# Spreading the norm's factor of each token over the partitions: by a store to DRAM and a repeating load, in the place of products of ones with diagonals

## The chip, the cores and the metric

The kernel runs on one core of one Trainium2 chip. The metric is the device time of one execution in microseconds (us); the kernel before takes 1041.21 us, the median of three runs (1041.09 to 1044.4).

## What is computed

One step of a hybrid decoder layer. A prompt of 2048 tokens and 8 single decode tokens, each of width 1024, go through one mixer that has two groups of heads on the same normalised input. What matters here is the first line of it: the norm, and the projections behind it.

```python
def rmsnorm(x, g):
    xf = x.astype(jnp.float32)
    y = xf * lax.rsqrt(jnp.mean(xf * xf, axis=-1, keepdims=True) + NORM_EPS)
    return (y * g.astype(jnp.float32)).astype(x.dtype)
...
def mixer_layer(x, pos, s_ret, s_hg, norm_g, w_in, ret_g, hg_g, lb, w_out):
    B, L, _ = x.shape
    h = rmsnorm(x, norm_g)
    p = (h @ w_in).astype(jnp.float32)
    rq, rk, rv, rg, hq, hf, hi, hgate = jnp.split(p, 8, axis=-1)
    ...
    y = x + o_cat @ w_out
```

Each token has one factor, 1/sqrt(mean(x*x) + eps). The activations lie transposed on the chip, with the width on the 128 partitions and the tokens along a row. A factor that belongs to a token is therefore the same on all partitions and changes along the row, while the sums of squares come out with one token on each partition. Bringing the factors from one layout into the other is what the change is about.

## The kernel before

**Pairs and steps.** The first 570 us project the 2048 tokens with three sets of weights. The tokens are cut into eight blocks of 256 (two chunks of 128). `TOK` lists 24 turns, eight for each set of weights; the program calls turn i "pair i", since it makes two chunks. Pairs 0 and 1 are plain products. From pair 2 on, `v_pair` (L393) makes a 2x2 block product out of seven smaller ones, in seven steps numbered 0 to 6 (`CHAIN`, L364). A step is 12 matmuls of 128x512: each float is split into a high and a low part (`hi_lo`, L114: ScalarE writes `ab_h`, VectorE writes `ab_l`), and high*high, high*low and low*high are added up. Of the names, `pv4a`, `pv4b`, `pv4c` are the PSUM banks of pair 4.

**What a pair needs.** `tok_load` (L235) brings the raw activations `xr` of a block, two halves of 512 KB. `tok_ops` (L306) multiplies them in place by the norm's gain and the spread factor `rb` (L313, eight instructions of 128x256), splits them into `ab_h` and `ab_l`, and makes four sums S1 to S4 (L328 to L331), which `s_split` (L338) splits into `s..h` and `s..l`. Scaled activations and sums are stored for the later sets (`a_dram` L321, `s_dram` L334). All this is done for pair i+1 while pair i is multiplied. What a pair makes leaves as `vo` (`emit`, L402): `vo440` after step 1 of pair 4, `vo451` after step 4 (a copy by ScalarE, L412, and an addition by VectorE, L413), `vo441` after step 5, `vo450` after step 6. Each goes out by a store to `v_dram` (L354).

**The factor before.** `stats_load` and `stats_sum` load the tokens once more, untransposed (`xn`), and square and sum them on ScalarE (L267). GpSimd adds the halves and takes the power -0.5 (L277, L111, L112); the result is a column of `rs_all` with one token on each partition. `spread_dg` (L284) makes two diagonal matrices `dg` of it on VectorE. `spread` (L290) multiplies ones by them on TensorE (L293, `prs`), so that every partition gets the row of factors, and VectorE copies the row out of PSUM to `rb` (L295). That is done for eight blocks: for pairs 2 to 7, each during the pair before it, and for pairs 10 and 11, which are the first to meet the blocks of the plain pairs. The eight decode tokens have their own small copy of the scheme (`decode_dg` L620, `decode_spread` L623).

**The gate.** In pairs 2 to 5 and 10 to 13 the weights of the next set are fetched as well: `wg_load` (L524) loads two tiles `wgr` of 512 KB in step 0. Behind step 4 TensorE multiplies the decode tokens by them (`wg_decode` L531, sixteen matmuls `pgd` at L600). TensorE works in the order of the program, so these matmuls hold step 5 until both loads have landed; they are called the gate of the pair below. VectorE then makes four sums of `wgr` (L513 to L516) and SyncE stores them (`ws1T`, L539).

**What sets the order.** TensorE's order is that of the program. On VectorE, ScalarE, GpSimd and SyncE a scheduler sets the order from its own estimate of when each operand is ready, and then the order is fixed: each engine takes its instructions one after the other, and one that waits holds all behind it. SyncE issues most of the DMAs (q1), GpSimd's queue (q0) the others. The function `past` keeps the diagonals behind the work of the pair before on VectorE.

Of the kernel before, what the change touches and what calls it, by code (L numbers as in the profile page):

```python
# [41 lines left out]
def step_kernel(ctx, tc, a, out):  # L42
# [232 lines left out]
    def stats_end(i):  # L275
        p, ms = V_ORDER[i], st[i]
        pool.tensor_tensor(ms[:, 0:2], ms[:, 0:2], ms[:, 2:4], op=ALU.add)  # L277
        rsqrt_mean(rs_all[:, 2 * p : 2 * p + 2], ms[:, 0:2], D, EPS)

    spread_to = {}  # L280

    dgs = {}

    def spread_dg(i):  # L284
        t = vq.tile([P, GW], F32, tag="rk", name=f"dg{i}")
        dgs[i] = [t[:, :P], t[:, P : 2 * P]]
        for dg, c in zip(dgs[i], (2 * TOK[i], 2 * TOK[i] + 1)):
            dve.tensor_scalar(dg, ident, rs_all[:, c : c + 1], None, op0=ALU.mult)

    def spread(i):  # L290
        pt = ps_tr.tile([P, 2, P], F32, tag="tr", name=f"prs{i}")
        for j, dg in enumerate(dgs[i]):
            pe.matmul(pt[:, j], ones, dg, start=True, stop=True)  # L293
# [4 lines left out]
    sop, lows = {}, {}  # L298

    def past(i, f):  # L300
        if i not in lows:
            return f()
        with tc.issue_after(lows[i]):
            f()

    def tok_ops(i, held=None):  # L306
        store = held.append if held is not None else lambda f: f()
# [16 lines left out]
        lows[i] = next(x for x in reversed(nc.cur_bb.bb.instructions) if x.engine == dve.engine)  # L324
# [263 lines left out]
    def decode_inputs():  # L588
        msd = sm.tile([NB, 2], F32, tag="msd", name="msd")
        for h in range(2):  # L590
            r = vq.tile([NB, GW], F32, tag="xn", name=f"xns{h}", bufs=2)
            sp.dma_start(r, a["x_sample"][:, h * GW : (h + 1) * GW])
            act.activation(r, r, AF.Square, accum_out=msd[:, h : h + 1])
        pool.tensor_tensor(msd[:, 0:1], msd[:, 0:1], msd[:, 1:2], op=ALU.add)
        rsqrt_mean(rsd[:, 1:2], msd[:, 0:1], D, EPS)
        pool.tensor_scalar(rsd[:, 0:1], rsd[:, 1:2], KSCALE, None, op0=ALU.mult)
    def four(ps, x, w, first, last):

        for j in range(4):
            pe.matmul(ps[32 * j : 32 * j + x.shape[1]], x, w[:, j * 256 : j * 256 + 256], start=first, stop=last)  # L600
# [17 lines left out]
    dgd = sm.tile([NB, NB], F32, tag="dgd", name="dgd", bufs=1)  # L618

    def decode_dg():  # L620
        dve.tensor_scalar(dgd, ident[:NB, :NB], rsd[:, 1:2], None, op0=ALU.mult)

    def decode_spread():  # L623
        pt = ps_tr.tile([P, NB], F32, tag="tr", name="prsd")
        pe.matmul(pt, ones[:NB, :], dgd, start=True, stop=True)
# [64 lines left out]
    tok_load(2)  # L690
    wv_comb(2)
    wv_comb(3)
    spread_dg(2)
    for ty in (1, 0):
        for c in range(2):
            ps = bank([P, GW], f"pv1{c}{ty}")
            for k in range(KT):
                plain_k(1, ps, c, ty, k, k == 0, k == KT - 1)
            plain_out(1, c, ty, ps)
            if (c, ty) == (0, 0):  # L700
                spread(2)
# [216 lines left out]
    for i in range(2, n_tok):  # L918
# [15 lines left out]
                sop[i + 1, op] = sop[i, op]  # L934
        elif i + 1 < n_tok:
            if not spooled(i + 1):
                after[0] += [lambda i=i: past(i, lambda: spread_dg(i + 1))]
                after[1] += [lambda i=i: spread(i + 1)]
            tied = behind if i >= N_V - 1 else lambda f: f()
            late = 2 if same(i) else 0  # L940
            after[2 + late] += [
                lambda i=i, t=tied: t(lambda: tok_ops(i + 1)), lambda i=i, t=tied: t(lambda: s_split(i + 1, 0))
            ]
            after[4 + late // 2] += [lambda i=i, t=tied: t(lambda: s_split(i + 1, 1))]
# [11 lines left out]
            after[4] += [lambda i=i: rot_load(i + 1)]  # L956
        if i == 2:
            after[3] += [lambda: behind(decode_values_out)]
            after[0] += [decode_dg]
            after[2] += [decode_spread]  # L960
        if m < 3:
            if 2 <= j < 6:
                after[0] += [lambda m=m, k=j - 2: wg_load(m, k)]
# [1020 lines left out]
```

## Time and profile before

| | before |
|---|---|
| median of three runs | 1041.21 us |
| span of the profiled execution, first to last instruction | 1040.8 us |
| TensorE busy | 1028.0 us, 99% |
| VectorE busy | 746.6 us, 72% |
| ScalarE busy | 554.1 us, 53% |
| GpSimd busy | 125.8 us, 12% |
| data moved by DMA | 255.61 MB, 246 GB/s on average |
| the product that spreads a factor (`prs`, L293) | 32 matmul records, 4.9 us |
| the diagonals (`dg`, L288) | 16 instructions, 4.1 us |
| the copy to `rb` (L295) | 8 instructions, 3.3 us |

The time of the profiled execution by itself is not listed; its span is 0.4 us under the median of the runs. The granted TensorE clock was 0.998 on average. The profile gives a busy time to every engine; TensorE's is long because matmuls overlap, so a wait of TensorE is read in the timeline, where a row says how long the engine was idle before it and who ended that.

### The profile page before, as it was taken

The page shows a single profiled execution, that of the slowest core. Times are in us where ns is not written, and L with a number is a line of the kernel's source. Part 1 is how long each engine was busy: PE and PEld are TensorE (multiplying, and loading weights), DVE is VectorE, ACT ScalarE, POOL GpSimd, SP SyncE. Part 2 cuts the span into 40 slices and gives each one's busy share as a digit, 9 for nine tenths or more (in the row PEclk, how much of TensorE's full clock was granted, in tenths as well). Part 3 has the DMA queues.
Part 4 walks back from the last instruction along what each step waited for, and adds up shares of the span by engine and source line. Part 5 has one row for each costly group of instructions (what it writes and reads, how often), then busy time and mean ns, then how long its engine had stood idle before and what let it go on. Part 6 is the DMA issues. An engine that isn't in the chain of part 4 may idle for free.

```text
span 1040.8 us, 21338 instructions
## 1 busy us (share of the span) xinstructions
PE 1028.0 (99%) x8231; PEld 851.5 (82%) x8231; DVE 746.6 (72%) x1387; ACT 554.1 (53%) x1209; POOL 125.8 (12%) x231
## 2 busy tenths in 40 slices
PE   9999999999999999999999999999999999999997
PEld 7778778787778888888888889898878888888775
DVE  6886676888665876666665767868767676667886
ACT  7853345635435765545554756565555465533242
POOL 0210001000000111111111100111022112312122
PEclk9999999999999999999999999999999999999999
DMA  8689999679998975487775696754785195575652
GB/s 298 214 325 336 321 335 310 266 252 318 312 333 301 366 248 161 163 274 218 231 255 165 244 321 212 259 161 161 236 255 189 36 382 206 161 286 187 240 183 102
DMA packets 151270, 255.61 MB, mean 246 GB/s; under 512 B 11424, under 2 KB 79280, under 8 KB 151040
## 3 DMA queue, kind: packets, MB, share of 16 engines
q1 hardware_dynamic: 143584, 229.22, 65.2%
q0 software_dynamic: 7440, 24.76, 6.2%
q8 instruction: 65, 1.06, 0.4%
q14 instruction: 37, 0.30, 0.1%
q10 hardware_dynamic: 144, 0.26, 0.1%
HBM read 166.51 MB, written 87.69 MB: 244 GB/s over the span
## 4 chain that ended last, share of the span: by engine, by line
PE 87%; DMA 6%; ACT 3%; DVE 2%; issue 1%; SPq 1%; POOL 0%; POOLq 0%; ACTq 0%; DVEq 0%
PE po L360 11%; PE pjqh L1039 9%; PE pjfh L1039 9%; PE py L1662 4%; PE plh L1255 2%; DMA xn<-in_x_prompt 2%; PE poh L1142 1%; PE par L744 1%; PE puh L1126 1%; PE pur L751 1%; PE por L757 1%; DMA T3l<-ws1T 1%; PE poh L1144 1%; PE por L759 1%; PE pv20a L360 1%
## 5 line engine op out<-in xcount | busy, mean ns | idle before, releaser
L1039 PE MATMUL pjfh<-xh,w_h 128*128 128x512 f32 (+2 forms) x160 | 59.9, 375 | 0.0
L1039 PE MATMUL pjqh<-xh,w_h 128*128 128x512 f32 (+2 forms) x160 | 59.8, 374 | 0.0
L1235 ACT ACTIVATE kepth<-kh 128x1024 f32<-128x1024 f32 x24 | 25.4, 1060 | 62.8 <-DVE kh L1225 62.7
L1039 PE MATMUL pjqh<-xh,w_l 128*128 128x512 f32 (+2 forms) x160 | 55.8, 349 | 0.0
L1039 PE MATMUL pjfh<-xl,w_h 128*128 128x512 f32 (+2 forms) x160 | 55.7, 348 | 0.0
L1039 PE MATMUL pjfh<-xh,w_l 128*128 128x512 f32 (+2 forms) x160 | 55.7, 348 | 0.0
L1039 PE MATMUL pjqh<-xl,w_h 128*128 128x512 f32 (+2 forms) x160 | 55.7, 348 | 0.0
L1225 DVE TENSOR_TENSOR kh<-kh,fph 128x512 f32<-128x512 f32 x48 | 33.4, 696 | 25.2 <-PE plh L1255 15.0
L116 DVE TENSOR_TENSOR ab_l<-xr,ab_h 128x512 fp32r<-128x512 f32 (+1 forms) x40 | 37.3, 954 | 6.6 <-ACT ab_h L115 6.6
L782 DVE SCALAR_TENSOR_TENSOR obr<-por,omr,rg 128x128 f32<-128x128 f32 x64 | 18.0, 345 | 32.3 <-POOL omr L774 27.6
L115 ACT ACTIVATE ab_h<-xr 128x512 fp32r<-128x512 f32 (+1 forms) x40 | 32.4, 840 | 15.2 <-DVE xr L313 15.2
L772 ACT ACTIVATE obr<-por 128x128 f32<-128x128 f32 x64 | 16.8, 277 | 43.4 <-PE por L759 41.1
L419 ACT ACTIVATE vo<-vo 128x512 f32<-128x512 f32 x32 | 20.1, 629 | 27.3 <-DVE vo L413 13.7
L1039 PEld LDWEIGHTS pjqh<-xh,w_h 128*128 128x128 f32 x160 | 30.2, 188 | 5.1 <-issue 1.6
L1039 PEld LDWEIGHTS pjqh<-xh,w_l 128*128 128x128 f32 x160 | 30.1, 188 | 4.1
L1039 PEld LDWEIGHTS pjfh<-xh,w_l 128*128 128x128 f32 x160 | 30.1, 188 | 4.1
L1039 PEld LDWEIGHTS pjfh<-xh,w_h 128*128 128x128 f32 x160 | 30.2, 189 | 3.8
L1228 DVE TENSOR_TENSOR qqh<-qqh,fph 128x512 f32<-128x512 f32 x48 | 32.8, 683 | 0.0
L313 DVE SCALAR_TENSOR_TENSOR xr<-xr,g_in,rb 128x256 f32<-128x256 f32 x64 | 27.0, 480 | 7.8 <-issue 5.0
L1039 PEld LDWEIGHTS pjqh<-xl,w_h 128*128 128x128 f32 x160 | 30.2, 189 | 2.7
L1039 PEld LDWEIGHTS pjfh<-xl,w_h 128*128 128x128 f32 x160 | 30.3, 189 | 2.7
L1157 DVE SCALAR_TENSOR_TENSOR obh<-poh,orsh,v 128x128 f32<-128x128 f32 x64 | 18.0, 344 | 13.4 <-POOL orsh L112 13.4
(1840 smaller groups left out, 3385.6 us busy)
## 6 DMA issues: line engine op xcount, KB each, us to landing
xr<-a_dram SPq DMA_DIRECT2D x24, 512.0 KB, 5.5
S<-s_dram SPq DMA_DIRECT2D x24, 512.0 KB, 5.6
xn<-in_x_prompt SPq DMA_DIRECT2D x32, 256.0 KB, 3.6
xr<-in_x_t SPq DMA_DIRECT2D x16, 512.0 KB, 6.1
a_dram<-xr SPq DMA_DIRECT2D x16, 512.0 KB, 4.1
s_dram<-S SPq DMA_DIRECT2D x16, 512.0 KB
wgr<-in_w SPq DMA_DIRECT2D x16, 512.0 KB, 8.7
xr<-a_dram SPq DMA_DIRECT2D x32, 256.0 KB, 4.4
```

The lines of the kernel that those rows point to most:

```text
L115: act.activation(h, src, AF.Copy)
L116: dve.tensor_tensor(l, src, h.bitcast(F32), op=ALU.subtract)
L313: dve.scalar_tensor_tensor(r[:, k], r[:, k], g_in[:, kk : kk + 1], spread_to[i], op0=ALU.mult, op1=ALU.mult)
L360: pe.matmul(ps, xx, ww, start=(first and n == 0), stop=(last and n == 2), skip_group_check=more)
L419: act.activation(o, src, AF.Silu)
L782: dve.scalar_tensor_tensor(o[:, cc], po[:, h], ms[:, h : h + 1], rb_of[c, "g"][:, cc], op0=ALU.mult, op1=ALU.mult)
L1039: pe.matmul(ps, ww[:, kk], x[:, k, b0 : b0 + n], start=(k == 0 and i == 0), stop=(k == KT - 1 and i == 2),)
L1225: dve.tensor_tensor(kv[:, :, 0, :], kv[:, :, 0, :], two[:, :, 1:2].to_broadcast([P, nb, b]), op=ALU.mult)
L1228: dve.tensor_tensor(qv[:, :, 1, :], qv[:, :, 1, :], two[:, :, 0:1].to_broadcast([P, nb, b]), op=ALU.mult)
L1235: act.activation(ss[:, 512:], k[:, :HALF], AF.Copy)
L1255: pe.matmul(dst[32 * i : 32 * i + 32, c], kk, qq, start=True, stop=True)
L1662: pe.matmul(ps, o[:, kk], w[:, k % 4, i * 512 : (i + 1) * 512], start=(k == 0 and n == 0), stop=(k == KT - 1 and n == 2),)
```

## The change

GpSimd stores each block's factors to DRAM as soon as it has them (`stats_end`, and `decode_inputs` for the decode tokens). `spread` becomes one DMA on SyncE's queue, which reads the 256 factors as one row of 1 KB and writes it to all 128 partitions of `rb`. Diagonals, products and copies are gone. The place in the program at which a spread is asked for stays step 0 or 1 of the pair before; for the decode tokens the multiplication of `xs` becomes a function of its own.

```diff
+    rs_dram = [dr.tile([2, P], F32, tag=f"rs_dram{p}", name=f"rs_dram{p}") for p in range(8)]
+    rsd_dram = dr.tile([1, NB], F32, tag="rsd_dram", name="rsd_dram")
...
         rsqrt_mean(rs_all[:, 2 * p : 2 * p + 2], ms[:, 0:2], D, EPS)
+        if i >= 2 or p in TOK[:2]:
+            pool.dma_start(rs_dram[p].rearrange("c t -> t c"), rs_all[:, 2 * p : 2 * p + 2])
...
-    def spread_dg(i):
-        t = vq.tile([P, GW], F32, tag="rk", name=f"dg{i}")
-        dgs[i] = [t[:, :P], t[:, P : 2 * P]]
-        for dg, c in zip(dgs[i], (2 * TOK[i], 2 * TOK[i] + 1)):
-            dve.tensor_scalar(dg, ident, rs_all[:, c : c + 1], None, op0=ALU.mult)
-
     def spread(i):
-        pt = ps_tr.tile([P, 2, P], F32, tag="tr", name=f"prs{i}")
-        for j, dg in enumerate(dgs[i]):
-            pe.matmul(pt[:, j], ones, dg, start=True, stop=True)
         dst = vq.tile([P, GW], F32, tag="rq", name=f"rb{i}")[:, :256]
-        dve.tensor_copy(dst, pt.rearrange("p a b -> p (a b)"))
+        sp.dma_start(dst, rs_dram[TOK[i]].rearrange("c t -> (c t)").partition_broadcast(P))
         spread_to[i] = dst
...
+        pool.dma_start(rsd_dram.rearrange("o b -> b o"), rsd[:, 1:2])
...
     def decode_spread():
-        pt = ps_tr.tile([P, NB], F32, tag="tr", name="prsd")
-        pe.matmul(pt, ones[:NB, :], dgd, start=True, stop=True)
         rb = sm.tile([P, NB], F32, tag="rbd", name="rbd", bufs=1)
-        act.activation(rb, pt, AF.Copy)
-        dve.tensor_tensor(xs, xs, rb.unsqueeze(1).to_broadcast([P, KT, NB]), op=ALU.mult)
+        sp.dma_start(rb, rsd_dram[0].partition_broadcast(P))
+        dec_rb.append(rb)
...
             if not spooled(i + 1):
-                after[0] += [lambda i=i: past(i, lambda: spread_dg(i + 1))]
-                after[1] += [lambda i=i: spread(i + 1)]
+                after[0] += [lambda i=i: spread(i + 1)]
```

The scheduler then gives the engines another order. Three places of it follow; the number behind a name tells allocations apart.

**VectorE, pair 4.** `xr50` and `xr51` are the two halves of pair 5's activations, `vo451` is what pair 4 makes in its step 4. Before:

```order
L415 TENSOR_TENSOR vo440_1185<-pv4b_1172,s1_4_1163 128x512
L295 COPY rb5_1191<-prs5_1188 128x256
L313 SCALAR_TENSOR_TENSOR xr50_1127<-xr50_1127,g_in_162,rb5_1191 128x256 x4
L313 SCALAR_TENSOR_TENSOR xr51_1128<-xr51_1128,g_in_162,rb5_1191 128x256 x2
L116 TENSOR_TENSOR ab_l_188<-xr50_1127,ab_h_187 128x512
L313 SCALAR_TENSOR_TENSOR xr51_1128<-xr51_1128,g_in_162,rb5_1191 128x256 x2
L328 TENSOR_TENSOR S1_5_1222<-xr50_1127,xr51_1128 128x512
L330 TENSOR_TENSOR S0_5_1221<-xr50_1127 128x512
L116 TENSOR_TENSOR ab_l_188<-xr51_1128,ab_h_187 128x1024
L329 TENSOR_TENSOR S0_5_1221<-S1_5_1222,xr50_1127 128x512
L413 TENSOR_TENSOR vo451_1267<-vo451_1267,p5_4_1253 128x512
```

And now:

```order
L401 TENSOR_TENSOR vo440_1178<-pv4b_1165,s1_4_1157 128x512
L399 TENSOR_TENSOR vo451_1255<-vo451_1255,p5_4_1241 128x512
L300 SCALAR_TENSOR_TENSOR xr50_1121<-xr50_1121,g_in_171,rb5_1159 128x256 x4
L300 SCALAR_TENSOR_TENSOR xr51_1122<-xr51_1122,g_in_171,rb5_1159 128x256 x2
L118 TENSOR_TENSOR ab_l_197<-xr50_1121,ab_h_196 128x512
L300 SCALAR_TENSOR_TENSOR xr51_1122<-xr51_1122,g_in_171,rb5_1159 128x256 x2
L499 TENSOR_TENSOR wgr12_1161<-wgr12_1161 128x512
L314 TENSOR_TENSOR S1_5_1210<-xr50_1121,xr51_1122 128x512
```

`vo451`, which needs the end of step 4, stood behind the scaling of pair 5's activations and now stands ahead of it. Pairs 3 and 5 read alike; in pairs 2, 6, 9 and 10 the scaling keeps its place ahead of that addition.

**SyncE, from the end of pair 3 to pair 4's scaled activations.** `vo3150` is what pair 3 makes last; `wgr12` and `wgr16` are the weights of pair 4's gate. Before:

```order
L354 DMA v_dram11_96<-vo3141_1124 128x512
L240 DMA xr50_1127<-in_x_t 128x1024
L240 DMA xr51_1128<-in_x_t 128x1024
L261 DMA xn00_1131<-in_x_prompt 128x512
L261 DMA xn01_1132<-in_x_prompt 128x512
L354 DMA v_dram10_95<-vo3150_1147 128x512
L527 DMA wgr12_1168<-in_w_1 128x1024
L527 DMA wgr16_1170<-in_w_1 128x1024
```

And now:

```order
L340 DMA v_dram11_96<-vo3141_1118 128x512
L242 DMA xr50_1121<-in_x_t 128x1024
L242 DMA xr51_1122<-in_x_t 128x1024
L263 DMA xn00_1125<-in_x_prompt 128x512
L263 DMA xn01_1126<-in_x_prompt 128x512
L340 DMA v_dram10_95<-vo3150_1141 128x512
L288 DMA rb5_1159<-rs_dram3_110 128x256
L513 DMA wgr12_1161<-in_w_1 128x1024
L513 DMA wgr16_1163<-in_w_1 128x1024
```

The load of the spread factors has come in ahead of the gate's weights. Further up, before and now, stand the stores of pair 4's scaled activations and sums, which wait for VectorE.

**ScalarE, ahead of pair 2.** `xr20` and `xr21` are pair 2's halves, `xn150` and `xn151` tokens whose squares are summed. Before:

```order
L267 ACTIVATE xn141_705,ms7_708<-xn141_705 128x512
L638 ACTIVATE vp100_666<-pv100_641,rs_all_170 128x512
L267 ACTIVATE xn150_711,ms7_708<-xn150_711 128x512
L267 ACTIVATE xn151_712,ms7_708<-xn151_712 128x512
L115 ACTIVATE ab_h_187<-xr20_554 128x512
L115 ACTIVATE ab_h_187<-xr21_555 128x1024
```

And now:

```order
L269 ACTIVATE xn141_711,ms7_714<-xn141_711 128x512
L117 ACTIVATE ab_h_196<-xr20_566 128x512
L623 ACTIVATE vp100_677<-pv100_652,rs_all_179 128x512
L269 ACTIVATE xn150_717,ms7_714<-xn150_717 128x512
L117 ACTIVATE ab_h_196<-xr21_567 128x1024
L269 ACTIVATE xn151_718,ms7_714<-xn151_718 128x512
```

The two `ab_h` stood behind both sums of squares and now come earlier.

More of the change, by code (lines that the diff above doesn't have):

```diff
@@ L278, in stats_end @@
         rsqrt_mean(rs_all[:, 2 * p : 2 * p + 2], ms[:, 0:2], D, EPS)
+        if i >= 2 or p in TOK[:2]:
+            pool.dma_start(rs_dram[p].rearrange("c t -> t c"), rs_all[:, 2 * p : 2 * p + 2])
     spread_to = {}
[L282 to L288 removed]
     def spread(i):
[L291 to L293 removed]
         dst = vq.tile([P, GW], F32, tag="rq", name=f"rb{i}")[:, :256]
[L295 removed]
+        sp.dma_start(dst, rs_dram[TOK[i]].rearrange("c t -> (c t)").partition_broadcast(P))
         spread_to[i] = dst
[L298 to L304, printed above, removed]
+    sop = {}
     def tok_ops(i, held=None):
@@ L323, in tok_ops @@
             return
-        lows[i] = next(x for x in reversed(nc.cur_bb.bb.instructions) if x.engine == dve.engine)
         a11, a21, a12, a22 = r0[:, :, :P], r0[:, :, P:], r1[:, :, :P], r1[:, :, P:]
@@ L692, in step_kernel @@
     wv_comb(3)
-    spread_dg(2)
+    spread(2)
     for ty in (1, 0):
@@ L700, in step_kernel @@
             if (c, ty) == (0, 0):
-                spread(2)
                 held = []
@@ L958, in step_kernel @@
             after[3] += [lambda: behind(decode_values_out)]
-            after[0] += [decode_dg]
-            after[2] += [decode_spread]
+            after[0] += [decode_spread]
+            after[2] += [decode_scale]
         if m < 3:
```

6 lines of the change are left out of this document (3 added, 3 removed).

## The prediction

> **What bounds the kernel now.** I read the busy times and the chain of work that ended last, then the stretches of the first 250 us, then the timelines of each engine around one pair.
>
> ```profile
> PE 1028.0 (99%) x8231; PEld 851.5 (82%) x8231; DVE 746.6 (72%) x1387; ACT 554.1 (53%) x1209; POOL 125.8 (12%) x231
> PE 87%; DMA 6%; ACT 3%; DVE 2%; issue 1%; SPq 1%; POOL 0%; POOLq 0%; ACTq 0%; DVEq 0%
> ```
>
> TensorE is the bound of the program: 87% of the chain is its own. Whatever shortens or stretches its work in the first 250 us is carried to the end, unless another limit stands there. The stretches (TensorE, weight loads, VectorE, ScalarE, GpSimd, then clock, DMA share, GB/s) show one:
>
> ```profile
> 80.00:100.00 20.00, 20.00 (x103) 15.83 (x102) 15.06 (x26) 7.69 (x13) 0.00 (x0) 1.00 0.94 339
> 100.00:120.00 20.00, 19.48 (x99) 15.10 (x98) 12.85 (x24) 9.01 (x17) 1.08 (x3) 1.00 0.95 349
> 120.00:140.00 20.00, 19.29 (x99) 14.99 (x98) 13.89 (x25) 7.97 (x16) 1.08 (x3) 1.00 0.94 346
> 200.00:250.00 50.00, 50.00 (x246) 40.68 (x245) 43.67 (x77) 22.01 (x33) 0.00 (x0) 1.00 0.73 259
> ```
>
> From 80 to 140 us (pairs 3 to 5) the DMA engines are 94 to 95% busy and TensorE idles a little; from 200 us on it doesn't. TensorE's timeline tells what it idles for:
>
> ```profile
> 56.53 0.50 PE L360 MATMUL pv2a<-wv_h,ab_h 128*128 128x512 f32 x1 [0.82 <-ACT ab_h L115]
> 60.51 0.50 PE L360 MATMUL pv2b<-wv_h,ab_l 128*128 128x512 f32 x1 [0.27 <-DVE ab_l L116]
> 115.34 0.62 PE L600 MATMUL pgd<-wgr,pk 128*8 128x256 f32 x8 [0.45 <-DMA wgr<-in_w]
> 137.00 0.62 PE L600 MATMUL pgd<-wgr,pk 128*8 128x256 f32 x8 [0.71 <-DMA wgr<-in_w]
> ```
>
> The gates of pairs 4 and 5 already wait for their weights. So two things have to be worked out: what TensorE gains, and what becomes of the gates.
>
> **What goes.** The chain of work, in order of time (start, length, what):
>
> ```profile
> 66.67 0.31 PE prsd L625 x2
> 66.98 2.97 PE pv2c L360 x12
> 69.95 2.72 PE pv2a L360 x12
> 72.67 0.98 PE pgd L600 x16
> 73.65 2.97 PE pv2c L360 x12
> ...
> 82.05 2.73 PE pv3b L360 x12
> 84.78 0.45 PE prs L293 x4
> 85.23 2.77 PE pv3a L360 x12
> ...
> 93.43 0.98 PE pgd L600 x16
> 94.41 2.98 PE pv3c L360 x12
> ```
>
> A spread takes 0.45 us of TensorE, and the step behind it 2.77 in the place of 2.72: 0.50 us. Eight of them and the decode tokens' 0.31 are 4.3 us. The diagonals and copies that VectorE loses, and ScalarE's copy for the decode tokens, I cost at nothing: VectorE waited for TensorE or GpSimd around them. TensorE's waits of 0.82 and 0.27 at pair 2 should go as well, since the first `ab_h` no longer stands behind sums of squares that wait for loads. By the gate of pair 2 that makes 2 x 0.50 + 0.31 + 0.82 + 0.27 = 2.4 us. Its weights are asked for a little earlier too, so I let it keep this: it ends at 73.65 - 2.4 = 71.25. Step 4 of pair 3 then ends at 93.43 - 2.4 - 0.5 = 90.5.
>
> **What moves.** In pairs 3 to 5 VectorE now finishes `vo..51` (after step 4) before it begins to scale the next pair. Rows of pair 4, before:
>
> ```profile
> 109.64 2.47 DVE L313 SCALAR_TENSOR_TENSOR xr<-xr,g_in,rb 128x256 f32<-128x256 f32 x6 [2.97 <-issue]
> 112.02 0.69 DVE L116 TENSOR_TENSOR ab_l<-xr,ab_h 128x512 fp32r<-128x512 f32 x1
> ...
> 116.48 0.68 DVE L413 TENSOR_TENSOR vo<-vo,p 128x512 f32<-128x512 f32 x1
> ...
> 117.69 1.23 DVE L116 TENSOR_TENSOR s50l<-S,s50h 128x1024 fp32r<-128x1024 f32 x1
> ...
> 114.50 0.58 ACT L412 ACTIVATE vo<-pv4a 128x512 f32<-128x512 f32 x1
> ```
>
> Copy and addition take 0.58 + 0.68, about 1.3 us; eight scalings at 0.41 are 3.3, and `ab_l` adds 0.6. So `ab_l` is there 5.2 us after step 4, while the gate and steps 5 and 6 take 0.98 + 2.98 + 2.72: nothing that step 0 needs is late. What is late is SyncE. VectorE's block per pair, from the scaling to the last sum of the weights, lasts this long (0.7 of it is the addition that moves ahead):
>
> ```profile
> 109.64:123.24 13.60, 13.47 (x22) 1.00 0.92 352
> ```
>
> Behind it SyncE issues the last store of sums and of `vo..41`, then the loads of the pair after, then the gate's weights:
>
> ```profile
> 122.07 1.80 SPq L539 DMA_DIRECT2D ws1T<-wgr  x4
> 123.91 0.76 SPq L354 DMA_DIRECT2D v_dram<-vo  x1
> 124.71 1.55 SPq L240 DMA_DIRECT2D xr<-in_x_t  x2
> 126.36 0.87 SPq L261 DMA_DIRECT2D xn<-in_x_prompt  x2
> 127.28 0.85 SPq L354 DMA_DIRECT2D v_dram<-vo  x1
> 128.22 1.28 SPq L527 DMA_DIRECT2D wgr<-in_w  x2
> ...
> 128.92 8.04 DMA wgr<-in_w
> ```
>
> (The last row is from the chain: the second of these weights landed at 136.96.) From the load of `xr` to the weights' landing 136.96 - 124.71 = 12.3 us pass. So after the change, from the end of step 4 of a pair to the end of the *next* pair's gate:
>
> - 1.3 copy by ScalarE and addition by VectorE
> - 12.9 VectorE's block without the addition (13.6 - 0.7)
> - 0.9 two stores issued
> - 12.3 loads and weights, as above
> - 0.5 the load of `rb` ahead of the weights: 0.4 to issue, 128 KB to move
> - 0.5 for the wait on the store of the factors (below)
> - 0.6 the gate's last eight matmuls
>
> That is 29.0 us. Before, it was 115.34 + 0.62 - 93.43 = 22.5, with the wait, since VectorE's block ran beside steps 2 to 4. TensorE alone needs 0.98 + 2.98 + 6 x 2.72 + 0.98 = 21.3. Now the gates, one by one:
>
> - Pair 3: VectorE's order in pair 2 is hardly changed, and the weights are asked for behind one load more; I take 94.0, against 94.41.
> - Pair 4: 90.5 + 29.0 = 119.5, against 116.0.
> - Pair 5: step 4 of pair 4 ends at 94.0 + 2.98 + 6 x 2.72 = 113.3. VectorE would come to its first sum of `wgr` 5.2 us later, at 118.5, and waits for the late gate of pair 4 until 119.5. 113.3 + 29.0 + 1.0 = 143.3, against 137.6: 5.7 us late.
>
> Behind that three spreads remain to be saved (in pairs 6, 9 and 10), 1.5 us. Sum: +5.7 - 1.5 = **+4.2 us**. Against the span of 1040.8 and the 0.4 to the median of the runs, I forecast 1045.4.
>
> **What the trace does not show.** No store of 256 separate words, and no load that repeats a row. The nearest:
>
> ```profile
> rot<-in_rot SPq DMA_DIRECT2D x16, 128.0 KB, 4.9
> d_dram<-de POOLq DMA_DIRECT2D x8, 2.0 KB, 1.6
> T3l<-ws1T POOLq DMA_DIRECT2D x2, 512.0 KB, 13.5
> ...
> 106.51 1.12 SPq L527 DMA_DIRECT2D wgr<-in_w  x2
> ...
> 102.98 0.19 POOL L277 TENSOR_TENSOR ms<-ms 128x2 f32<-128x2 f32 x1 [24.50 <-ACT xn L267]
> 103.54 0.69 POOL L112 TENSOR_TENSOR rs_all<-rs_all,mhalf 128x2 f32<-128x2 f32 x1
> ```
>
> The load of `rb` is like that of `rot`, 128 KB on the same queue: 4.9 us, behind what the queue holds. It is asked for some 5 us before VectorE wants it, so it costs its place in the queue alone. The store lies between 1.6 us (2 KB from GpSimd) and 13.5 (512 KB under load); I take 2.5, near the small one, and keep both ends. GpSimd has nothing behind it for 20 us. SyncE has: the load of `rb` waits for the store, and the gate's weights stand behind it. The factors come at about 104.2 in pair 4, and SyncE reached the weights at 106.5, so it may stand for some 2 us, all the more as ScalarE's order now puts pair 4's first copy ahead of the sums of squares. The megabyte of `xr` ahead of the weights is still moving then; that hides most of it, and I count 0.5. Without that cover it is 2.
>
> **Rivals.**
>
> *The store lands late.* At 6.5 us, about midway, SyncE stands 4 us longer, of which some 1.5 is still covered: +2.5 at pair 5, 1047.9. For it: nothing in the trace is like 256 words. Against: the 1.6 us. [...] Chance 0.10.
>
> *The queue has room, and the gates fall back to about where they were.* VectorE is still late, but the stores that used to share the queue with the loads are now bunched elsewhere, so that 12.3 becomes some 9.5: loop 26, pair 5's gate at 113.3 + 26 = 139.3, +1.7 - 1.5, 1041.4. For it: the queue runs empty while VectorE waits for step 4. Against: the 94% busy engines. Chance 0.22.
>
> *Faster: the gates don't hold.* TensorE's gain comes out whole if the loop stays under about 22 us, because transfers that begin earlier at pair 2 (2.4 us) keep their lead through pair 5. The gain would be 4.3 + 1.1 at pair 2 + the gates' 0.45 + 0.71, that is 6.6, and half of it by a loop of 23: 1034.6 to 1038. Against: VectorE's 12.9 us behind step 4 leave 21.3 - 1.3 - 12.9 = 7 for everything on SyncE's side. Chance 0.13.
>
> *VectorE itself becomes late for step 2*: `s50l` ended 117.69 + 1.23 - 109.64 = 9.3 us after the scaling began; with the addition away, two sums of `wgr` ahead of it and the 1.3 it comes 11 us after step 4, and step 2 of the next pair at 0.98 + 2.98 + 3 x 2.72 = 12.1. If the scaling starts 2 us late in three pairs, TensorE loses some 5 more: 1050. Chance 0.05.
>
> **How the numbers follow.** The forecast has 0.50 and reaches from 1043.0 (a loop of 27) to 1048 (31). A measurement of this kernel tells about 0.3%, 3.1 us, from no change: slower means over 1044.3, and of the forecast's half some 0.38 lies there and 0.12 within. Slower: 0.38 + 0.10 + 0.05 = 0.53. The same: 0.12 + 0.22 = 0.34. Faster 0.13. The range leaves out the whole gain below and the worst of the late cases above: 1039.5 to 1050.
>
> **What would show it.** Right: `prs` gone; the wait of 0.82 at pair 2 gone; step 5 of pair 2 starting near 71; VectorE idle some 6 us in step 2 to 4 of pairs 3 to 5; waits at `pgd` for `wgr` of 3 to 5 us in pairs 4 and 5; from 200 us on TensorE unbroken. Wrong: no longer waits at those gates (then it is faster), waits of `rb`'s load on the store beyond 3 us, or a wait of TensorE for `s..l`.

## The result, and the profile after

| | before | after |
|---|---|---|
| median of the runs | 1041.15 us (four runs) | 1128.37 us (four runs) |
| ratio | | 1.083, 95% interval 1.0816 to 1.0844 |
| span of the profiled execution | 1040.8 us | 1126.2 us |
| first matmul of pair 2 | 56.5 us | 75.2 us |
| first matmul of pair 4 | 99.9 us | 143.3 us |
| first matmul of pair 6 | 143.1 us | 211.3 us |
| first matmul of pair 8 | 181.7 us | 256.3 us |
| first matmul of pair 16 | 349.3 us | 428.7 us |

The changed kernel is 87 us slower. The starts of the pairs say where: 74.6 of the 85.4 us of the span are lost by the start of pair 8, some 12 us per pair from pair 2 to pair 6, while factors are still being spread. First the page: busy times, then the chain that ended last, by engine and by line.

```profile
PE 1043.3 (93%) x8197; PEld 852.7 (76%) x8197; DVE 740.2 (66%) x1362; ACT 553.7 (49%) x1208; POOL 133.7 (12%) x240
...
PE 68%; DMA 18%; DVE 6%; ACT 3%; issue 2%; POOL 1%; SPq 1%; POOLq 0%; ACTq 0%; DVEq 0%
PE po L346 10%; PE pjqh L1022 8%; PE pjfh L1022 8%; DMA rs_dram<-rs_all 6%; PE py L1645 3%; DMA xn<-in_x_prompt 3%; DMA wgr<-in_w 2%; PE plh L1238 2%; DVE xr L300 2%; PE par L728 1%; PE poh L1125 1%; PE pur L735 1%; PE por L741 1%; DMA or<-o_dram 1%; PE puh L1109 1%
```

DMA has gone from 6% to 18% of the chain, and a transfer of 1 KB, the store of the factors, is a third of that. The stretches that stand in the prediction now read (TensorE, weight loads, VectorE, ScalarE, GpSimd, clock, DMA share, GB/s):

```profile
80.00:100.00 20.00, 11.67 (x50) 9.21 (x48) 4.24 (x6) 5.53 (x11) 1.90 (x2) 0.84 0.83 192
100.00:120.00 20.00, 18.87 (x86) 14.00 (x87) 14.45 (x24) 8.50 (x15) 3.83 (x4) 0.89 0.92 272
120.00:140.00 20.00, 8.58 (x41) 5.30 (x40) 7.42 (x14) 2.89 (x4) 0.00 (x0) 0.74 0.83 203
200.00:250.00 50.00, 42.97 (x181) 32.90 (x182) 27.16 (x46) 19.14 (x32) 4.36 (x9) 0.90 0.70 237
```

TensorE is busy for 8.6 to 18.9 of 20 us, and the DMA engines, nearly as busy as before, move 192 to 272 GB/s in the place of 339 to 349. A busy share that stays while the bytes fall means that packets take longer: from 80 to 100 us a KB costs a DMA engine 69 ns (0.83 x 16 / 192), where it cost 44 (0.94 x 16 / 339). TensorE's timeline has the waits (the last column):

```profile
75.19 0.80 PE L346 MATMUL pv2a<-wv_h,ab_h 128*128 128x512 f32 x1 [18.53 <-ACT ab_h L117]
100.88 1.04 PE L587 MATMUL pgd<-wgr,pk 128*8 128x256 f32 x8 [9.21 <-DMA wgr<-in_w]
134.47 1.04 PE L587 MATMUL pgd<-wgr,pk 128*8 128x256 f32 x8 [11.12 <-DMA wgr<-in_w]
168.66 1.04 PE L587 MATMUL pgd<-wgr,pk 128*8 128x256 f32 x8 [11.47 <-DMA wgr<-in_w]
202.29 1.04 PE L587 MATMUL pgd<-wgr,pk 128*8 128x256 f32 x8 [10.96 <-DMA wgr<-in_w]
234.42 0.80 PE L346 MATMUL pv7a<-wv_h,ab_h 128*128 128x512 f32 x1 [3.71 <-ACT ab_h L117]
```

These six make 65.0 us. Every gate from pair 2 to pair 5 waits, for 9 to 11 us. One turn of the loop, from the chain in order of time (start, length, what; pieces of `issue` under 0.1 us are left out), ends at the gate of pair 3:

```profile
108.51 1.33 ACT xn L269 x4
109.92 1.14 POOL ms L279
111.15 0.69 POOL rs_all L113
111.91 1.26 POOL rs_all L114
113.17 0.40 issue
113.56 13.85 DMA rs_dram<-rs_all
127.43 0.33 SPq L288
127.81 0.42 SPq L513
128.28 7.49 DMA wgr<-in_w
```

The store of the factors is issued at 113.56 and lands 13.85 us later. SyncE stands behind it with the load of `rb` (L288), and the gate's weights (L513) are the next thing on its queue. SyncE's waits on that store, in all (us in total, times, longest):

```profile
SPq L288 <- DMA rs_dram<-rs_all: 60.7, 6, 11.9
```

The store's issue-to-landing times over all eight, least, median and most:

```profile
DMA to landing us min/median/max: 8.6/9.6/13.9
```

And it isn't only late itself. Two stretches around the first store, which is issued at 28.6 us, after:

```profile
30.00:34.00 4.00, 4.00 (x43) 2.35 (x41) 3.97 (x9) 2.87 (x7) 0.00 (x0) 1.00 1.20 45
34.00:38.00 4.00, 4.00 (x22) 3.12 (x18) 1.73 (x3) 0.00 (x0) 0.00 (x0) 1.00 0.76 21
```

and before:

```profile
30.00:34.00 4.00, 4.00 (x43) 2.30 (x42) 3.96 (x8) 3.05 (x7) 0.00 (x0) 1.00 0.87 286
34.00:38.00 4.00, 4.00 (x19) 3.33 (x18) 3.91 (x7) 4.00 (x9) 2.17 (x3) 1.00 0.90 290
```

At 28 to 38 us nobody waits for the store by a semaphore, and yet everything that the core transfers falls from 290 GB/s to 21. That gave three theories. **A**: the small words stall all the core's transfers. **B**: what costs is SyncE's standing on the wait, and what is queued behind. **C**: GpSimd's queue is slow in this place, whatever it carries. Besides, the forecast's own reckoning (the order, +4.2 us) was to be tried without a store.

### The profile page after: what moved, and what is told of

Its sections match the earlier page's. It is cut to its first block, busy times and chain, and to the rows that moved or that the text cites. A ratio compares the mean times of both kernels' runs of the same rounds, so it can differ in the third digit from the quotient of the medians.

```text
span 1126.2 us, 21269 instructions
## 1 busy us (share of the span) xinstructions
PE 1043.3 (93%) x8197; PEld 852.7 (76%) x8197; DVE 740.2 (66%) x1362; ACT 553.7 (49%) x1208; POOL 133.7 (12%) x240
## 4 chain that ended last, share of the span: by engine, by line
PE 68%; DMA 18%; DVE 6%; ACT 3%; issue 2%; POOL 1%; SPq 1%; POOLq 0%; ACTq 0%; DVEq 0%
PE po L346 10%; PE pjqh L1022 8%; PE pjfh L1022 8%; DMA rs_dram<-rs_all 6%; PE py L1645 3%; DMA xn<-in_x_prompt 3%; DMA wgr<-in_w 2%; PE plh L1238 2%; DVE xr L300 2%; PE par L728 1%; PE poh L1125 1%; PE pur L735 1%; PE por L741 1%; DMA or<-o_dram 1%; PE puh L1109 1%
## 5 line engine op out<-in xcount | busy, mean ns | idle before, releaser
L587 PE MATMUL pgd<-wgr,pk 128*8 128x256 f32 x128 | 12.7, 497 | 44.1 <-DMA wgr<-in_w 44.1
L756 ACT ACTIVATE obr<-por 128x128 f32<-128x128 f32 x64 | 16.9, 278 | 44.1 <-PE por L743 41.8
L269 ACT ACTIVATE xn<-xn 128x512 f32<-128x512 f32 x32 | 19.9, 622 | 36.4 <-DMA xn<-in_x_prompt 36.4
L399 DVE TENSOR_TENSOR vo<-vo,p 128x512 f32<-128x512 f32 x21 | 14.5, 688 | 30.6 <-ACT vo L398 30.0
L405 ACT ACTIVATE vo<-vo 128x512 f32<-128x512 f32 x32 | 20.1, 630 | 26.6 <-DVE vo L399 11.4
```

Of the source, the lines that this page charges most:

```text
L269: act.activation(r, r, AF.Square, accum_out=st[i][:, 2 * h + j : 2 * h + j + 1])
L405: act.activation(o, src, AF.Silu)
```

## The experiments

All were timed in three rounds beside the kernel before on the same chip. The third column is the ratio to it with its 95% interval.

| run | median us | ratio | stores land after, us (median) |
|---|---|---|---|
| the change | 1128.4 | 1.083 (1.0816 to 1.0844) | 9.6 |
| e1: before, plus the word stores, unread | 1077.6 | 1.0339 (1.0318 to 1.036) | 10.9 |
| e2: change, loads wait for no store | 1100.6 | 1.0564 (1.0532 to 1.0597) | 11.4 |
| e3: change, store of two rows of 512 B | 1082.2 | 1.0376 (1.0347 to 1.0406) | 4.6 |
| e4: e2 without stores | 1058.6 | 1.015 (1.0126 to 1.0174) | |
| e5: e1, 128 pieces of 8 B | 1054.0 | 1.0133 (1.0093 to 1.0172) | 8.3 |
| e6: e1, words 512 B apart | 1040.7 | 0.9989 (0.9978 to 1.0) | 4.8 |
| e7: e1, issued by SyncE | 1073.0 | 1.0299 (1.0283 to 1.0314) | 8 to 14 (all) |
| e8: e1, 128 pieces of 64 B | 1041.1 | 0.9993 (0.9982 to 1.0004) | 5.5 |
| e9: e4, loads asked for early | 1051.8 | 1.0106 (1.0087 to 1.0125) | |
| e10: e3, loads issued by GpSimd | 1087.1 | 1.0445 (1.0425 to 1.0465) | 4.3 |
| e11: before, plus the loads, unread | 1044.3 | 1.0028 (1.0013 to 1.0043) | |
| e12: change, pieces of 128 B, all computed | 1083.2 | 1.0399 (1.0373 to 1.0426) | 4.7 |
| e13: e12, sums of squares earlier | 1069.9 | 1.0274 (1.0239 to 1.031) | 3.2 |
| e14: change, words 512 B apart | 1079.1 | 1.036 (1.0332 to 1.0388) | 5.1 |

### Stall or wait: e1 to e4

e1 puts only the stores into the kernel before.

```diff
+    rs_dram = [dr.tile([2, P], F32, tag=f"rs_dram{p}", name=f"rs_dram{p}") for p in range(8)]
...
         rsqrt_mean(rs_all[:, 2 * p : 2 * p + 2], ms[:, 0:2], D, EPS)
+        if i >= 2 or p in TOK[:2]:
+            pool.dma_start(rs_dram[p].rearrange("c t -> t c"), rs_all[:, 2 * p : 2 * p + 2])
```

> The kernel before, spread by products as it was, with the eight word stores of the prompt's factors added on GpSimd (256 words of 4 B each); nobody reads what they write, and the order of every engine but GpSimd is that of before. Theory A (the words stall all transfers of the core for some 6 us each): the loads on SyncE's queue land late, xn takes about 10 us instead of some 4, and the time rises to 1060 to 1095 us. Theory B (only SyncE's wait for the store matters): nobody waits, 1041 us within 3.

Measured 1077.6: theory A. The same stretches as above, of this run:

```profile
30.00:34.00 4.00, 4.00 (x42) 2.31 (x41) 3.97 (x8) 2.92 (x7) 0.00 (x0) 1.00 1.35 51
34.00:38.00 4.00, 4.00 (x19) 3.31 (x18) 1.47 (x3) 0.00 (x0) 0.00 (x0) 1.00 0.39 16
```

Nobody reads what is stored, nobody waits for it, every other engine has its old order, and the core's transfers fall to 16 GB/s all the same. TensorE has lost 34.6 us at the start of pair 6, and 34.3 at the end: the loss lies where the stores lie.

e2 takes the wait from the change and leaves the stores:

```diff
-        sp.dma_start(dst, rs_dram[TOK[i]].rearrange("c t -> (c t)").partition_broadcast(P))
+        sp.dma_start(dst, a["x_sample"][0, 0:256].partition_broadcast(P))
...
-        sp.dma_start(rb, rsd_dram[0].partition_broadcast(P))
+        sp.dma_start(rb, a["x_sample"][0, 0:8].partition_broadcast(P))
```

> The changed kernel with its word stores, but the repeating loads read a row of the input x_sample in the place of the stored factors, so that they wait for no store (the scaled activations are those of another factor). Theory A (stall of all transfers by the words): the stores still stall the loads, 1060 to 1100 us. Theory B (SyncE standing on the wait): the wait is gone, 1042 to 1046 us.

1100.6, just above theory A's range and 55 us above that of B. The wait is worth something too: 1128.4 - 1100.6 = 28 us (with another order, since the scheduler then puts the loads elsewhere).

e3 keeps wait and order, and changes the shape of the store:

```diff
+    pool.memset(row[0:1, 0:P], 1.0)
...
-            pool.dma_start(rs_dram[p].rearrange("c t -> t c"), rs_all[:, 2 * p : 2 * p + 2])
+            pool.tensor_copy(row[0:1, 0:2], rs_all[0:1, 2 * p : 2 * p + 2])
+            pool.dma_start(rs_dram[p].unsqueeze(0), row[0:1, 0:P].unsqueeze(1).to_broadcast([1, 2, P]))
```

> The changed kernel with the same wait, but the store writes two rows of 512 B from one partition (two words of it are factors, the rest a constant, so the scaled activations are those of another factor); every engine but GpSimd has the order of the changed kernel. Theory A: such a store lands within 3 us of its issue and stalls nobody, and the time falls to 1043 to 1052 us. Theory B: SyncE still waits, but for some 2.5 us in the place of 9 to 13, about 1046 to 1055. Theory C (a store of GpSimd's queue lands slowly whatever it carries): landing after 8 to 14 us, about 1120 us.

1082.2: 46 us go, so C falls, for the same queue lands this store in 1.7 to 5.8 us. But 30 us more remain than theory A had said. That was the first miss: without any stall, the wait and the way through DRAM still cost.

e4 is e2 without its stores:

```diff
-        if i >= 2 or p in TOK[:2]:
-            pool.dma_start(rs_dram[p].rearrange("c t -> t c"), rs_all[:, 2 * p : 2 * p + 2])
...
-        pool.dma_start(rsd_dram.rearrange("o b -> b o"), rsd[:, 1:2])
```

> The run with free loads without any store of factors: what is left of the change is the products gone, the repeating loads added and the new order (the scaled activations are those of another factor). The forecast's reckoning of the order: +4.2 us, about 1045. If the queue has room, as in one of its rivals: 1041 or less; if TensorE's gain comes out whole: 1035 to 1038. Its difference to the run with free loads and stores is the price of the stores alone: some 20 to 55 us by theory A, within 3 by theory B.

1058.6: the stores are worth 42 us here (1100.6 - 1058.6). But with no store and no wait the change still costs 16 us, not the 4.2 of the forecast. VectorE's rows say for what it waits:

```profile
93.72 2.46 DVE L300 SCALAR_TENSOR_TENSOR xr<-xr,g_in,rb 128x256 f32<-128x256 f32 x6 [6.74 <-DMA rb<-in_x_sample]
115.64 2.46 DVE L300 SCALAR_TENSOR_TENSOR xr<-xr,g_in,rb 128x256 f32<-128x256 f32 x6 [6.61 <-DMA xr<-in_x_t]
```

It waits 6 to 7 us for transfers on SyncE's queue, the load of `rb` among them.

### What of the store stalls: e5 to e8

All four are e1 with another store: the same eight moments, unread, and (but for e7) every other engine in the same order.

```diff
-[2, P]   pool.dma_start(rs_dram[p].rearrange("c t -> t c"), rs_all[:, 2 * p : 2 * p + 2])
+[P, 2]      e5: pool.dma_start(rs_dram[p], rs_all[:, 2 * p : 2 * p + 2])
+[2, P, P]   e6: pool.dma_start(rs_dram[p][:, :, 0].rearrange("c t -> t c"), rs_all[:, 2 * p : 2 * p + 2])
+[2, P]      e7: sp.dma_start(rs_dram[p].rearrange("c t -> t c"), rs_all[:, 2 * p : 2 * p + 2])
+[P, 16]     e8: pool.dma_start(rs_dram[p], rs_all)
```

(The shape is that of the DRAM tile; e7 stands in `spread`.)

> The kernel before with unread stores, as the run with words only (which cost 35.0 us), but each store goes in 128 pieces of 8 B, side by side in DRAM, in the place of 256 words of 4 B: the same 1 KB. Theory N (the count of pieces sets the stall): half of 35 us, about 1060. Theory L (pieces that fall into the same short stretch of DRAM hold each other up): still eight pieces to a stretch of 64 B, somewhere between 1055 and 1078. Theory G (GpSimd's queue itself is slow in this place): unchanged, 1075 to 1080.

> The same with 256 words of 4 B, but each word 512 B away from the next in DRAM. Theory L (neighbouring words hold each other up): the stall goes, 1041 to 1048. Theory N (the count of pieces): unchanged, 1073 to 1082. Theory G: unchanged.

> The same 256 words to neighbouring addresses, but issued by SyncE, one step after the pair's begin, when the factors have long been there; two of the eight stores then fall into pairs 9 and 10. Theory G (GpSimd's queue): the stall goes, 1041 to 1046. Theories L and N (the words themselves): six stores up to pair 7 still stall, about 1062 to 1080, and the store lands 8 us or more after its issue.

> The same on GpSimd's queue with 128 pieces of 64 B (all sixteen columns of the factors, 8 KB; two of them mean something). Theory N: like the pieces of 8 B, about 1060. Theory L (each piece has a stretch of 64 B for itself): 1041 to 1048. Theory G: unchanged, 1075 to 1080.

e7 (1073.0) ends theory C (G in these expectations) for good: SyncE's queue lands the words as late, 8 to 14 us after the issue, and stalls as much: from 46 to 54 us the core's transfers run at 66 and 0 GB/s, where the kernel before has 211 and 199. (The scheduler moved the two stores of pairs 9 and 10 to 41 us, so all eight lie ahead of 190 us, unlike what the expectation says.) The other three tell the count from the place. e5 costs 12 us, a third of e1 and somewhat less than either theory had said; e6 and e8 cost nothing. The first store again, pieces of 8 B side by side (e5):

```profile
30.00:34.00 4.00, 4.00 (x42) 2.33 (x41) 3.96 (x9) 2.70 (x5) 0.00 (x0) 1.00 0.96 55
34.00:38.00 4.00, 4.00 (x19) 3.27 (x19) 1.56 (x3) 1.11 (x3) 0.00 (x0) 1.00 0.81 291
```

256 words of 4 B, each 512 B from the next (e6):

```profile
30.00:34.00 4.00, 4.00 (x43) 2.31 (x41) 3.97 (x9) 3.32 (x8) 0.00 (x0) 1.00 0.72 218
34.00:38.00 4.00, 4.00 (x22) 3.31 (x19) 3.81 (x7) 3.64 (x10) 2.03 (x4) 1.00 0.90 302
```

128 pieces of 64 B side by side (e8):

```profile
30.00:34.00 4.00, 4.00 (x43) 2.31 (x42) 3.96 (x9) 3.28 (x7) 0.00 (x0) 1.00 0.75 236
34.00:38.00 4.00, 4.00 (x18) 3.31 (x19) 3.50 (x7) 3.38 (x9) 1.83 (x4) 1.00 0.90 322
```

The stall lasts both stretches with neighbouring words, one with pieces of 8 B, and isn't there with the same number of words apart from each other, nor with pieces of 64 B. The count of pieces doesn't set it (e6 has as many as e1 and costs nothing), nor does their size alone (4 B in e6). Small writes to neighbouring addresses do (35 us in e1, 12 in e5), theory L. Distances between 4 and 512 B and sizes between 8 and 64 B were not run, so where the stall ends, and what it is that neighbouring words share, is not known; the stretch of 64 B in the expectations was the author's assumption, which no run shows. (The profile can't tell the stores apart by its packets: it counts 32 to a store of GpSimd's queue in e1, e5, e6 and e8 alike.)

### What the wait costs: e9 to e13

e9 is e4 with each load of `rb` asked for in step 4 of the pair before the one in which it was asked for, that is three of a pair's seven steps earlier:

```diff
     s_split(2, 1)
+    spread(3)
...
-            if not spooled(i + 1):
-                after[0] += [lambda i=i: spread(i + 1)]
+            if i + 2 < n_tok and not spooled(i + 2):
+                after[4] += [lambda i=i: spread(i + 2)]
```

> The run without stores (1058.6, 1.5% above the kernel before), whose repeating loads of a row of x_sample are asked for two steps before the pair that they belong to, more than half a pair earlier, so that VectorE never waits for them (the scaled activations are those of another factor). If the rest of 16 us comes from rb landing late behind SyncE's other transfers, as VectorE's waits of 5 to 7 us for it say: 8 us of it go, 1046 to 1051. If it comes from the new order or from the bytes of the loads themselves: 1056 to 1060. If TensorE's gain then comes out whole: 1036 to 1040.

1051.8, 0.8 us above the first case: 7 of the 16 us go, and VectorE's waits for `rb` fall from 17.6 us in e4 to a single one of 4.9. (The order of VectorE changed with it, so that the 7 us are the lateness of `rb` alone is not shown.) e11 puts the loads alone into the kernel before:

```diff
         dve.tensor_copy(dst, pt.rearrange("p a b -> p (a b)"))
+        t = vq.tile([P, GW], F32, tag="rk", name=f"rl{i}")
+        sp.dma_start(t[:, :256], a["x_sample"][0, 0:256].partition_broadcast(P))
```

> The kernel before with eight repeating loads of a row of x_sample added on SyncE's queue, one behind each product that spreads; nobody reads what they bring. If the bytes of the repeating loads and their place on the queue are part of the 16 us that are left without stores: 1044 to 1050. If they cost nothing, and the 16 us are the new order and the lateness of rb: 1040 to 1043.

1044.3, at the lower edge of the first case: the eight loads of 128 KB, with nobody waiting, cost about 2.5 us.

e10 moves the loads of e3 to GpSimd's queue, so that SyncE never stands behind a store of factors:

```diff
-        sp.dma_start(dst, rs_dram[TOK[i]].rearrange("c t -> (c t)").partition_broadcast(P))
+        pool.dma_start(dst, rs_dram[TOK[i]].rearrange("c t -> (c t)").partition_broadcast(P))
...
-        sp.dma_start(rb, rsd_dram[0].partition_broadcast(P))
+        pool.dma_start(rb, rsd_dram[0].partition_broadcast(P))
```

> The run with rows in the place of words (1082.2), whose repeating loads are issued by GpSimd right behind its store, so that SyncE never stands on the wait for it (again only two words of a row are factors). If SyncE's standing is what costs the 24 us over the run without stores: 1055 to 1062. If the way of the factor itself, store and load one after the other, is what VectorE waits for: 1078 to 1085.

1087.1: taking the wait off SyncE's queue gains nothing by itself. VectorE waits now:

```profile
77.12 3.26 DVE L302 SCALAR_TENSOR_TENSOR xr<-xr,g_in,rb 128x256 f32<-128x256 f32 x8 [11.46 <-DMA rb<-rs_dram]
...
162.43 2.47 DVE L302 SCALAR_TENSOR_TENSOR xr<-xr,g_in,rb 128x256 f32<-128x256 f32 x6 [10.39 <-DMA rb<-rs_dram]
```

Store and load, one behind the other, are the way of the factor, and it is too long wherever the wait stands. But this run changed the order too, so two more were made. e12 computes everything, without a single word:

```diff
+    pool.memset(row[:, 0:64], 1.0)
...
-            pool.dma_start(rs_dram[p].rearrange("c t -> t c"), rs_all[:, 2 * p : 2 * p + 2])
+            pool.tensor_copy(row[:, 0:2], rs_all[:, 2 * p : 2 * p + 2])
+            dve.transpose(row[:, 32:64], row[:, 0:32])
+            for c in range(2):
+                pool.dma_start(rs_dram[p][c].rearrange("(q t) -> q t", t=32), row[c : c + 97 : 32, 32:64])
```

> The changed kernel with the whole computation kept, but without single words: VectorE turns the factors in blocks of 32x32, so that GpSimd stores them in eight pieces of 128 B. No stall of the transfers: each store lands in 2 to 6 us, as that of rows did. If the words' stall is the cost and the rest the way of the factor through DRAM: 1078 to 1088, as with rows. If small pieces of 128 B stall as well: above 1100.

1083.2, as with rows. e13 asks for the sums of squares earlier:

```diff
-            after[1 if i == 2 else 2] += [... stats_sum(i + 2, 0) ..., ... stats_load(i + 2, 1)]
-            after[4] += [... stats_sum(i + 2, 1) ..., ... stats_end(i + 2)]
+            after[0] += [... stats_sum(i + 2, 0) ..., ... stats_load(i + 2, 1)]
+            after[1] += [... stats_sum(i + 2, 1) ..., ... stats_end(i + 2)]
...
-                after[5] += [lambda i=i: stats_load(i + 3, 0)]
+                after[2] += [lambda i=i: stats_load(i + 3, 0)]
```

> The run with pieces of 128 B (1083.2, whole computation), with the sums of squares of pairs 4 to 7 and their loads asked for two to three steps earlier in the pair, so that the factors are ready some 6 to 8 us earlier. If what is left (24 us over the run without stores) is the factor's way through DRAM, some 10 us where the products took 2, behind sums that come late: most of it goes, 1060 to 1068. If it is SyncE's standing on the wait: 1078 to 1086, since SyncE still stands behind each store.

1069.9: 13 of the 25 us to e4 go, a little more than half, which lies between the two cases, 2 us short of the first. SyncE's standing on the store falls from 22.3 us in six waits (e12) to 2.9 in three, while VectorE's waits for `rb` stay as long (28.1 and 29.2 us). That speaks for SyncE's standing having a part in the cost after all, since in e10 the wait had only moved; but e13 changes the order of SyncE's transfers too, so the part isn't told apart. The factors of pair 5 now lie in DRAM 10 us before their load is issued (the store lands at 109.8, by its semaphore), so the wait on the store is gone there. What is left there is another thing, in the chain ahead of the gate of pair 4 (L344 is the store of `vo`, L292 the load of `rb`, L517 the gate's weights):

```profile
118.69 0.61 ACT u L390
119.29 0.14 SPq L344
...
119.54 0.44 SPq L292
...
121.90 0.40 SPq L517
...
122.35 7.92 DMA wgr<-in_w
```

SyncE stands behind the store of a result of pair 4, and asks for the gate's weights only then.

### The stall in the change itself: e14

```diff
-    rs_dram = [dr.tile([2, P], F32, tag=f"rs_dram{p}", name=f"rs_dram{p}") for p in range(8)]
+    rs_dram = dr.tile([8, 2, P, P], F32, tag="rs_dram", name="rs_dram")
+    pool.dma_start(rs_dram[:, 0, 0:2], a["x_sample"][:, 0:256].rearrange("p (c t) -> p c t", c=2))
...
-            pool.dma_start(rs_dram[p].rearrange("c t -> t c"), rs_all[:, 2 * p : 2 * p + 2])
+            pool.dma_start(rs_dram[p, :, :, 0].rearrange("c t -> t c"), rs_all[:, 2 * p : 2 * p + 2])
...
-        sp.dma_start(dst, rs_dram[TOK[i]].rearrange("c t -> (c t)").partition_broadcast(P))
+        sp.dma_start(dst, rs_dram[TOK[i], 0, 0:2].rearrange("c t -> (c t)").partition_broadcast(P))
```

> The changed kernel itself, its wait kept and the order of its engines the same but for two neighbours on VectorE, with one thing changed: each of the 256 words goes 512 B away from the next in DRAM. The repeating load waits for the store and reads 1 KB in a row, which holds a row of x_sample but for two words (the scaled activations are those of another factor). If neighbouring words are the dominant cost of the change: the store lands in 3 to 7 us and the time falls to that of rows, 1078 to 1090. If the count of the words or GpSimd's queue is: 1120 or more.

1079.1, with the wait kept. Its stores land so:

```profile
DMA to landing us min/median/max: 3.0/5.1/6.2
```

So of the 87 us of the change, 49 (1128.4 - 1079.1) are the neighbouring words: their stall of all transfers, and the 4 to 8 us by which the store itself lands later, where everything waits for it. SyncE's standing on it falls from 60.7 us to 25.7, again in six waits.

## Why the prediction was wrong

The steps down from the change add up so: 1128.4 to 1079.1 by setting the words apart (49); to 1058.6 without store and wait (about 20, or 24 to 25 from e3 and e12); to 1051.8 with `rb` asked for early (7); and 11 over the kernel before remain, of which 5.7 have come up by the start of pair 8. The order of these steps is a choice, since each changes what the next one hides.

**What goes.** `prs` and its 0.50 us are gone as said. The waits of 0.82 and 0.27 at pair 2 did not go: 18.53 us stand in their place. The chain ahead of pair 2 holds two loads of `xn` of 10.18 and 9.24 us, which run into the stalls of the first two stores, and then the factors' own way: store 8.61, load of `rb` 5.44. With the words apart (e14) pair 2 starts 0.6 us later than before the change.

**The step that failed is the price of the store.** The prediction bounded it by 1.6 us (2 KB from GpSimd) and 13.5 (512 KB under load), took 2.5 because "near the small one" is where 1 KB seemed to lie, and counted 0.5 us for the wait on it. Measured: 8.6 to 13.9 us, the upper end. Bytes were the wrong scale: the same 1 KB lands in 1.7 to 5.8 us as two rows (e3) and in 3.0 to 7.5 with its words apart (e6). And the far end was not carried through: at 13.5 us SyncE, which reached the weights at 106.5 with the factors ready at 104.2, would have stood some 11 us in each of four pairs. SyncE did stand 60.7 us in six waits, and the gates' waits, 9.21 to 11.47 us, are of that size. The turn from the end of step 4 to the end of the next gate, forecast at 29.0 us, took 45.2, 47.6 and 47.4. The prediction's own sign of being wrong, waits of `rb`'s load on the store beyond 3 us, is what came. A range that takes in the bounds of an unknown cost would have reached beyond 1080.

**The cover and the load were mis-sized too.** The price of the store is not the whole: in e14 it lands in 3.0 to 6.2 us, within the 6.5 of the rival, and the turn still takes 29.5, 33.1 and 39.5 us, and the kernel is 38 us behind. The prediction counted 0.5 us a turn for SyncE's standing, with the factors ready 2.3 us before SyncE came to the weights. In e14 it stands 4.3 us on average and 7.7 at most, longer than any store takes to land: there SyncE is at the load before the store is even issued, so the factors come late themselves, and e13 wins 13 us by asking for them earlier. And "asked for some 5 us before VectorE wants it" did not hold for `rb`: VectorE waits 17.6 us for it in e4, without any store.

**"It costs its place in the queue alone"** was said of the load, and of the store only landing time was thought of. That a store of 1 KB takes the transfers of the whole core from 290 GB/s to 21 was in no rival. Together with the late landing that it brings it is the larger part, 49 of 87 us (e14); where nobody waits for the store it costs 35 (e1).

**The rival of the late store** had the right wait, SyncE standing on the store, with 6.5 us in the place of 9.6, 1.5 us of cover, 2.5 us in all and a chance of 0.10; it had no stall of other transfers. The runs don't tie the late landing to GpSimd: e7 issues the words from SyncE and they land as late (8 to 14 us), and e6 leaves them with GpSimd and they land in 3.0 to 7.5.

**What moves.** The gates wait for `wgr`, as forecast (in all four pairs, where the forecast had two), and e13's chain has the mechanism in the forecast's form: SyncE behind a store of `vo`, and the weights asked for behind that. Its size was not told apart. Without stores (e4) pair 6 starts 7.4 us late, against the forecast's 5.7 at the gate of pair 5, but there the scheduler had put VectorE's addition back behind the scaling, so the agreement is by chance: what VectorE waits for there is `rb` and `xr`. The new order by itself was not run.

**From 200 us on TensorE unbroken**: not quite. In e4 the delay is 8.6 us at pair 8, 10.2 at pair 16 and 16.9 at the end, and after the change it grows likewise, while e1, which keeps TensorE's old program, holds 34.6 from pair 6 to 34.3 at the end. VectorE, ScalarE and SyncE have the order of before in all of the second half. Two single waits are seen in e4 (0.85 us for a load of `rq`, 0.73 at an instruction that waits for nothing shown). Most of it is not a wait: the matmuls themselves follow each other more slowly. Two steps of pair 12, in the kernel before:

```profile
266.98 2.72 PE pv12a L360 x12
269.70 2.72 PE pv12b L360 x12
```

and in e9:

```profile
271.05 2.80 PE pv12a L346 x12
273.85 2.80 PE pv12b L346 x12
```

The matmuls that read `ab_h` and `ab_l` start every 233 ns in the place of 227, at a granted clock of 1.00 in both, and so they do in the change, e4 and e14. Matched one by one with those of the kernel before, such lengthenings of a few ns, of other matmuls too, add up to 5.3 to 5.5 us behind the start of pair 8 in each of these four runs, and to nothing in e1 and e11, which keep TensorE's old program. So about 5 us of each of these are neither store nor load nor wait. Why the matmuls are slower is open; the change also drops a few small tiles, which may move others on the chip, and that was not tried.

**The range's ends.** By the prediction's own rule for pair 5 a loop of 27 gives 1042.4 and one of 31 gives 1049.4, not 1043.0 and 1048; nothing else hangs on it.

No version here beats the kernel before. Even with loads that wait for no store and were asked for early (e9) the kernel is 10.7 us behind, about half of it in the slower matmuls, and the products cost TensorE 4.3 us in all.

## What to carry to other kernels

Look at the size of a small transfer's pieces and at where they land: stores of 1 KB in words of 4 B that lie next to each other in DRAM held the transfers of the core down to 16 to 103 GB/s for some 8 us (e1, from 30 and from 78 us; the same stretches of e6 have 218 to 373), while the same words 512 B apart, or pieces of 64 B, cost no time that can be measured (0.9989 in e6 and 0.9993 in e8). A value that goes through DRAM takes store plus load, here 2 to 6 us for the store where it doesn't stall (e3, e12, e14) and 4.1 to 4.6 for the load (e4), in the place of about 2.5 us through TensorE (before, in pair 4: factors at 104.2, `rb` copied by 106.7); no run here shows it pay, having the value ready earlier won 13 us (e13), and moving the wait to another queue won nothing (e10). A changed program can also change the pace of instructions that it doesn't touch (here matmuls every 233 ns in the place of 227), so compare the steps of the second half as well. When the price of an unknown operation is bounded by two rows far apart, work the whole kernel through at both ends before choosing one.

## What the runs showed of the hardware that was not expected

**Neighbouring small writes.** 256 words of 4 B side by side: 35 us for eight stores (e1). 128 pieces of 8 B: 12 us (e5). Words 512 B apart and pieces of 64 B: no difference that can be measured (0.9989 and 0.9993). The bytes that the profile counts as read from DRAM are the same before and in e1 (166.51 MB). Why neighbouring words stall is not shown by any run.

**The clock after a wait.** The granted clock falls to half in the six long waits, 2.6 to 5.3 us after TensorE's last matmul, and stays there for 3 to 5 us after TensorE begins again. After the change, the stretch around the gate of pair 2:

```profile
98.00:103.00 5.00, 1.87 (x16) 0.24 (x16) 3.67 (x9) 1.76 (x4) 0.00 (x0) 0.50 0.99 388
```

and the chain at the gate of pair 5:

```profile
203.56 1.04 PE pgd L587 x8
204.60 4.03 PE pv5c L346 x12
208.63 2.79 PE pv5a L346 x12
```

The first step behind a wait takes 4.03 us in the place of 2.97, and the gate's eight matmuls 1.04 in the place of 0.62. The stretches at half of these six waits last 3.41 us (one), 10.24 (four) and 20.48 (one), that is one, three and six times the shortest; what sets these lengths is not shown. Up to pair 8 some 10 us are lost beyond the 65.0 of the six waits (74.6 - 65.0), and the slow beginnings are of that size: behind the six waits TensorE is busy for 23.9 us at a granted 0.50, where matmuls of 128x512 start every 0.43 us in the place of 0.23. An estimate from these figures is some 11 us; it was not measured by itself.
